# Copying neighbourhood q and k out of PSUM in one ScalarE pass, with scaled minima for row maxima, and three pieces of preparation work put elsewhere

## The chip, the cores and the metric

The kernel runs on one core of one Trainium2 chip. The metric is the device time of one execution in microseconds; lower is better. Several executions were timed, and one more was run under the hardware profiler, which gives the rows shown below. The engines are PE (TensorE: matmuls and, as PEld, weight loads), DVE (VectorE), ACT (ScalarE), POOL (GpSimd) and SP (SyncE, which here only issues DMAs).

## The reference

One transformer block on 1024 tokens of width 1024, batch 1. The tokens form a grid of 16 rows by 64 columns.

```python
h = layer_norm(x)
proj = h @ w_in + b_in                       # 1024 x 4352
qa, ka, va, qb, kb, vb, ga, gb = split(proj)
y_na  = neighbourhood_attention(qa, ka, va, rpb) @ w_branch_na   # 8 heads of 64, 8 x 16 window, bias
y_swa = windowed_gqa_with_sink(qb, kb, vb, sink) @ w_branch_swa  # 8 heads of 64, |i-j| <= 128, rotary
mixed = sigmoid(ga) * y_na + sigmoid(gb) * y_swa
h = layer_norm(2**.25 * h + mixed @ w_out + b_out)
u = square(relu(h @ w_ff1 + b_ff1))          # width 4096
h = layer_norm(2**.25 * h + u @ w_ff2 + b_ff2)
```

In the windowed attention the softmax has one more logit for each head, the sink. Its row maximum is the larger of the scores' maximum and the sink.

## The kernel before

All is float32 outside. For accuracy each operand of a product is split in a high and a low part, and a product is three matmuls: high by high, high by low, low by high. The first half of the program uses the type fp32r, the feed-forward layers use fp16 parts. `PE` is meant to run without a pause: everything else (splitting weights, copying out of PSUM, softmax, norms) is laid beside the matmuls by hand, in the order in which the Python code issues it (`manual_schedule` for all five engines). Each engine works through its own list in that order, so an instruction that waits holds up all behind it on its engine.

The stages that the change touches, in order of time:

**Attention (about 85 to 400 us).** One generator, `fill`, yields the projection matmuls one at a time; `pump(n)` issues n of them. `steps(s, n)` is one step of attention: the scores of step s+2 (`part_a`), a quarter of the n pumped matmuls, the exponentials of s+2 (`part_e`), the low parts of s+1 and their DMA transpose (`part_l`), 45% of the matmuls, the product with v of step s-1 (`part_c`), and the rest. A head is four steps; heads 0 to 7 are windowed heads, 8 to 15 neighbourhood heads. Work with a delay is put in a list by `defer(k, f, ...)`: f is issued at the first `flush` after k more pumped matmuls, and a flush marked early takes only what is marked early.

`proj_na_qk(h, ...)` is the projection of one neighbourhood head's q and k, in two halves of 512 tokens. Each half is 24 matmuls into one PSUM bank with tag "mm" (two banks have that tag). Rows 0 to 63 of the bank are q, rows 64 to 127 are k. `evac` copies q out once and k twice on ACT (high parts), `evac2`, deferred by D_NA = 4 matmuls, makes the low parts on DVE out of the same bank, which is free only after that. The score of a tile is then two matmuls of 128 rows: `q` (high over low) with `kh` (high twice), and `q` with `kl` (low twice). `part_a` adds bias or mask on DVE and takes row maxima with one `tensor_tensor_reduce` for each of two tiles into `st`; a `tensor_scalar` makes the negated scaled maxima `nm` from them (with the sink from `snk8`), and ACT's exponential reads `nm` as its bias.

**Output product and first norm (about 565 to 670 us).** For each of eight groups g of 128 tokens: two times 24 matmuls (`out_mm`), the residual added and statistics on DVE (`out_evac`), then `ln1_norm(g)`: the power for 1/std on POOL (L1366), a product on POOL (L174), the normalisation `z` on ACT (L176). In group g+1 PE turns group g (`turn`, 8 transposes at L1377). Two POOL jobs stand between: `bound`, seven small operations that need one small matmul's sum and give the scale `g1s` that `turn_evac` reads, and `late(i)`, four 128x512 POOL operations (L1529) that prepare the residual rows of group i.

**First feed-forward layer (about 665 to 962 us).** 16 column blocks p, each seven products of 12 matmuls in the order of `STEPS`: 1, 2, 6, 5, 7, 3, 4 (a Strassen-like scheme, banks a, b and c). After 1, 6 and 5 ACT takes a snapshot `sn` of the bank (L1614), before the bank's next product may be added to it. Beside them ACT and DVE prepare weights up to seven products ahead (`prep_to`), and ACT squares a whole raw weight block (`squares1`, 128x2048) to find its scale. For the second layer's first column group the four raw weight blocks are loaded by `load2` and squared by `squares2`, at the products that `LOAD2` and `SQUARE2` name as (p, product); `umax` and `scale2` make the scale out of these.

Of the kernel before, what the change touches and what calls it, by code (L numbers as in the profile page):

```python
# [10 lines left out]
F32 = mybir.dt.float32  # L11
F32R = mybir.dt.float32r
# [4 lines left out]
P = 128  # L17
# [73 lines left out]
def encoder_block(ctx, tc, x, w_in, w_br, w_out, w_ff1, w_ff2, par, rows, rpbp,  # L91
# [4 lines left out]
    def b32(ap):  # L96
        return ap.bitcast(F32)
# [90 lines left out]
    nc.scalar.dma_start(ident, ident_d)  # L188
    prm = cp.tile([P, N_PAR], F32, name="prm")
    nc.sync.dma_start(prm, par)  # L190
    snk8 = cp.tile([P, 8], F32, name="snk8")

    def bound_sets():
        for t, v in ((ones, 1.0), (pw[:, 0:1], -0.5), (pw[:, 1:2], 0.5), (cv, W_TOP ** -2), (hx[:, 4:6], 0.5),
# [98 lines left out]
    def h_perm(part, k, half):  # L293
        return hT[:, part, k, half * 512:(half + 1) * 512]
# [17 lines left out]
    def gemm3_steps(ps, w, act):  # L312

        hi, lo = w[:2]
        for k in range(NK):
            for i, (a, b) in enumerate(((hi, 0), (hi, 1), (lo, 0))):
                yield
                PE.matmul(ps, a[:, k, :], act(b, k), start=(k == 0 and i == 0), stop=(k == NK - 1 and i == 2))  # L318
# [92 lines left out]

    def proj_na_qk(h, w, store):
        q = ap.tile([P, S], F32R, tag="q", name="q", bufs=3)
        kh = ap.tile([P, S], F32R, tag="kh", name="kh")
        kl = ap.tile([P, S], F32R, tag="kl", name="kl")
        store.append((q, kh, kl))
        bq, bk = prm[0:64, C_QK + h:C_QK + h + 1], prm[64:P, C_QK + h:C_QK + h + 1]
        for half in range(2):
            cs = slice(half * 512, (half + 1) * 512)
            ps = psum("mm")  # L420
            yield from gemm3_steps(ps, w, lambda part, k: h_perm(part, k, half))

            def evac(cs=cs, ps=ps):
                ACT.activation(q[0:64, cs], ps[0:64, :], AF.Identity, bias=bq, scale=1.0)
                ACT.activation(kh[64:P, cs], ps[64:P, :], AF.Identity, bias=bk, scale=1.0)
                ACT.activation(kh[0:64, cs], ps[64:P, :], AF.Identity, bias=bk, scale=1.0)

            def evac2(cs=cs, ps=ps):
                DVE.scalar_tensor_tensor(out=q[64:P, cs], in0=ps[0:64, :], scalar=bq, in1=b32(q[0:64, cs]),
                                         op0=ALU.add, op1=ALU.subtract)  # L430
                DVE.scalar_tensor_tensor(out=kl[64:P, cs], in0=ps[64:P, :], scalar=bk, in1=b32(kh[64:P, cs]),  # L431
                                         op0=ALU.add, op1=ALU.subtract)
                DVE.tensor_copy(kl[0:64, cs], b32(kl[64:P, cs]))
            defer(0, lambda: (evac(), defer(D_NA, evac2, early=step_now[0] >= 32)), early=True)


    mk = ap.tile([P, 640], F32, tag="mk", name="mk", bufs=1)
# [182 lines left out]
    def part_a(s):  # L620

        hd, t = heads[s // 4], s % 4
        (q, kh, kl), _, _, bias_of, sink_h, o_chunk, o_row = hd.get()
        if t == 0 and o_row == 0:
            sums_l[o_chunk] = ap.tile([P, 2, 8], F32, tag="sl", name="sl", bufs=3)
            sums_s[o_chunk] = ap.tile([P, 2, 8], F32, tag="sk", name="sk", bufs=3)
        st = ap.tile([P, 2], F32, tag="st", name="st", bufs=4)
        nm = sums_s[o_chunk][:, o_row // 64, 2 * t:2 * t + 2]
        e = ap.tile([P, 768], F32, tag="ss", name="ss", bufs=2)
        tiles, at = [], 0  # L630
        for i in range(2):
# [4 lines left out]
            PE.matmul(ps[:, :n], q[:, j * P:(j + 1) * P], kh[:, c0 * P:c1 * P], start=True, stop=False)
            PE.matmul(ps[:, :n], q[:, j * P:(j + 1) * P], kl[:, c0 * P:c1 * P], start=False, stop=True)
            DVE.tensor_tensor_reduce(out=e[:, at:at + n], in0=ps[:, :n], in1=bias_of(j), scale=1.0, scalar=NEG,
                                     op0=ALU.add, op1=ALU.max, accum_out=st[:, i:i + 1])
            tiles.append((at, n, c0))  # L640
            at += n
        if sink_h is None:
            DVE.tensor_scalar(out=nm, in0=st, scalar1=-0.125, scalar2=None, op0=ALU.mult)  # L643
        else:
            DVE.tensor_scalar(out=nm, in0=st, scalar1=snk8[:, sink_h:sink_h + 1],
                              scalar2=-0.125, op0=ALU.max, op1=ALU.mult)
        hd.pairs[t] = e, tiles, at, nm
        if s > 0:
            rope_step(nm[:, 0:1])

    def part_e(s):

        if s >= 64:
            return
        hd, t = heads[s // 4], s % 4
        e, tiles, n_all, nm = hd.pairs[t]
        _, _, _, _, sink_h, o_chunk, o_row = hd.get()
        hh = o_row // 64
# [136 lines left out]
    with tc.manual_schedule(engines=MANUAL):  # L795
# [38 lines left out]
        for i in range(2 * NK + LAG + HB):  # L834
# [698 lines left out]
    with tc.manual_schedule(engines=MANUAL):  # L1533
# [6 lines left out]
        bound_squares()  # L1540
        for g in range(3, NCG):
            late_load(g)
        late(2)
        for g in range(NCG):
            out_mm(g, 0, 0, 8)
            if 2 <= g + 1 < NCG:
# [40 lines left out]
            if g == 5:
                op_places("S1", "S2")
            if g:
# [345 lines left out]
        for n, (p, i) in enumerate(seq):  # L1935
# [345 lines left out]
```

## Time and profile before

| what | us |
|---|---|
| three timed executions | 1263.60, 1264.92, 1265.20; median 1264.92 |
| the profiled execution: its own time | 1264.63 |
| the profiled execution: span from first to last instruction | 1262.8 |
| busy time of PE / DVE / ACT / POOL | 1235.7 / 960.0 / 797.0 / 321.3 |
| mean granted TensorE clock | 0.997 of full speed |

The profiled execution's own time is 1.8 us more than its span. A row of the timeline is: start, length in us, engine, line, operation, output<-inputs, shape, count; in brackets, how long the engine idled before it and what it waited for. A matmul's modelled end lies behind the start of the next one, since they are pipelined: what a matmul costs in a stream is the distance from its start to the next start.

### The profile page before, as it was taken

To read this page: it belongs to the slowest core of one execution; us is meant where nothing else is said; L and a number is where in the kernel's file an instruction comes from. 1 tells how busy PE (TensorE), PEld (TensorE's weight loads), DVE (VectorE), ACT (ScalarE), POOL (GpSimd) and SP (SyncE) were. 2 spreads that over 40 slices of the span, in tenths; PEclk is the share of its full clock that TensorE was granted. 3 is DMA by queue.
4 is the path that set the end of the run, shared out by engine and by line. 5 is a ranking of instruction groups with operands and counts; after the bars stand their busy time and mean duration, and the time that the engine had idled before them with its cause. 6 is when DMAs were issued, how large, how long until landed. Compare 5 with 4: busy or idle time off the path is not lost.

```text
span 1262.8 us, 16643 instructions
## 1 busy us (share of the span) xinstructions
PE 1235.7 (98%) x5954; PEld 796.4 (63%) x5954; DVE 959.9 (76%) x1409; ACT 797.0 (63%) x1280; POOL 321.3 (25%) x314
## 2 busy tenths in 40 slices
PE   8999999999999999999999999999999999999997
PEld 6788887877778778887884444444444444444443
DVE  7667889778778984443788977877757777898888
ACT  6448878677665455432567877787777746434457
POOL 4352331313110002436530013432300002211217
PEclk9999999999999999999999999999999999999999
DMA  6435667465476236546333456666927635363333
GB/s 238 158 143 132 153 152 176 105 159 131 110 165 200 73 134 202 199 133 243 124 150 109 138 188 217 209 204 205 335 90 266 226 134 225 125 257 127 125 109 133
DMA packets 166066, 211.55 MB, mean 168 GB/s; under 512 B 110432, under 2 KB 112224, under 8 KB 159712
## 3 DMA queue, kind: packets, MB, share of 16 engines
q1 hardware_dynamic: 165152, 209.72, 51.8%
q8 instruction: 46, 0.75, 0.2%
q10 hardware_dynamic: 832, 0.79, 0.2%
q14 instruction: 36, 0.29, 0.1%
HBM read 128.59 MB, written 56.18 MB: 146 GB/s over the span
## 4 chain that ended last, share of the span: by engine, by line
PE 72%; DVE 12%; ACT 7%; issue 3%; POOL 3%; DMA 2%; SPq 1%; POOLq 0%; DVEq 0%; ACTq 0%
PE ps_mm L318 17%; PE ps_o L1516 6%; PE ps_s L1986 6%; PE ps_mm L1986 6%; PE ps_t L1516 5%; PE ps_mm L1516 5%; PE ps_t L1986 5%; PE ps_o L1986 5%; PE ps_o L746 2%; PE ps_s L1516 2%; PE ps_mm L979 2%; PE ps_o L310 1%; PE ps_o L309 1%; PE ps_t L310 1%; PE ps_t L309 1%
## 5 line engine op out<-in xcount | busy, mean ns | idle before, releaser
L318 PE MATMUL ps_mm<-hT,whi 128*128 128x512 f32 x832 | 269.7, 398 | 7.1 <-DVE kl L431 4.5
L1516 PEld LDWEIGHTS <-tw 128*128 128x128 f16 x1248 | 122.5, 99 | 148.3 <-issue 5.8
L318 PEld LDWEIGHTS ps_mm<-hT,whi 128*128 128x128 f32 x832 | 155.2, 188 | 41.4 <-ACT ss L661 3.9
L1986 PEld LDWEIGHTS <-hS 128*128 128x128 f16 x1008 | 98.7, 98 | 118.2
L318 PE MATMUL ps_mm<-hT,wlo 128*128 128x512 f32 x416 | 165.5, 398 | 1.0 <-DVE wlo L812 1.0
L661 ACT ACTIVATE ss<-ss,sk 128x384 f32<-128x384 f32 (+1 forms) x128 | 74.3, 582 | 58.9 <-DVE sk L643 34.9
L1516 PE MATMUL ps_t<-hS,tw 128*128 128x512 f16 x384 | 88.1, 379 | 0.2
L318 PEld LDWEIGHTS ps_mm<-hT,wlo 128*128 128x128 f32 x416 | 78.3, 188 | 14.0 <-DVE wlo L812 1.5
L1271 POOL TENSOR_TENSOR mx<-sg 128x512 f32<-128x512 f32 x16 | 33.5, 2096 | 175.6 <-DVE sg L1270 175.6
L1704 DVE TENSOR_TENSOR usl<-usl 128x512 f32<-128x512 f32 x64 | 52.5, 821 | 27.1 <-ACT usl L1632 26.9
L1437 POOL TENSOR_TENSOR c<-c 128x2 f32<-128x2 f32 x16 | 16.8, 1056 | 199.3 <-DVE c L1436 199.3
L2006 POOL TENSOR_TENSOR acc<-acc,rst 128x512 f32<-128x512 f32 x16 | 32.8, 2051 | 121.5 <-DMA rst<-xr_d 113.7
L1986 PEld LDWEIGHTS <-hA 128*128 128x128 f16 x336 | 32.8, 98 | 39.7
L673 DVE SCALAR_TENSOR_TENSOR pl<-ss,pl 128x640 f16<-128x640 f32 (+1 forms) x64 | 57.1, 892 | 0.6 <-ACT pl L664 0.3
L1819 DVE SCALAR_TENSOR_TENSOR hS<-stg,c,hS 128x2048 f16<-128x2048 f32 x21 | 49.9, 2378 | 7.6 <-ACT hS L1816 7.6
L1443 DVE SCALAR_TENSOR_TENSOR tw<-raw,c,tw 128x512 f16<-128x512 f32 x60 | 51.1, 852 | 5.9 <-ACT tw L1440 5.9
L664 ACT ACTIVATE pl<-ss 128x640 f16<-128x640 f32 (+1 forms) x64 | 50.6, 791 | 3.0 <-DMA pt<-pl 1.0
L746 PE MATMUL ps_o<-pt,vv 128*128 128x256 f16 (+1 forms) x448 | 49.8, 251 | 0.0
L1516 PE MATMUL ps_o<-hS,tw 128*128 128x512 f16 x192 | 45.4, 388 | 2.1 <-ACT sn L1614 2.1
L444 POOL TENSOR_SCALAR tb<-tb 128x384 f32<-128x384 f32 x8 | 11.1, 1386 | 140.1 <-DMA tb<-in_rpbp 74.0
L1440 ACT ACTIVATE tw<-raw,c 128x512 f16<-128x512 f32 x60 | 41.4, 709 | 2.8 <-DVE raw L1481 2.8
L1986 PE MATMUL ps_mm<-hA,hS 128*128 128x512 f16 x192 | 42.9, 379 | 0.0
(386 smaller groups left out, 3001.2 us busy)
## 6 DMA issues: line engine op xcount, KB each, us to landing
us_d<-usl SPq DMA_DIRECT2D x112, 256.0 KB, 3.1
stg<-us_d SPq DMA_DIRECT2D x28, 1024.0 KB, 4.9
raw<-in_w_in SPq DMA_DIRECT2D x28, 512.0 KB, 4.0
raw<-in_w_ff SPq DMA_DIRECT2D x24, 512.0 KB, 5.7
sg<-sg_d SPq DMA_DIRECT2D x32, 256.0 KB, 3.0
hA<-in_w_ff SPq DMA_DIRECT2D x8, 1024.0 KB, 8.3
hS<-in_w_ff SPq DMA_DIRECT2D x8, 1024.0 KB, 8.1
sg_d<-sa SPq DMA_DIRECT2D x16, 256.0 KB, 2.3
```

What stands on the lines that cost most here:

```text
L318: PE.matmul(ps, a[:, k, :], act(b, k), start=(k == 0 and i == 0), stop=(k == NK - 1 and i == 2))
L661: ACT.activation(p, p, AF.Exp, bias=nm[:, i:i + 1], scale=0.125, accum_out=sums_l[o_chunk][:, hh, 2 * t + i:2 * t + i + 1])
L664: ACT.activation(pl[:, 0:n_all], e[:, 0:n_all], AF.Copy, bias=0.0, scale=P_SCALE)
L673: DVE.scalar_tensor_tensor(out=pl[:, n:2 * n], in0=e[:, 0:n], scalar=P_SCALE, in1=pl[:, 0:n], op0=ALU.mult, op1=ALU.subtract)
L746: PE.matmul(o, vs, move(part), start=(m == 0 and part == 0), stop=(m == len(runs) - 1 and part == 1))
L1271: POOL.tensor_tensor(out=mx[:, f, half * 512:(half + 1) * 512], in0=both[0], in1=both[1], op=ALU.add)
L1440: ACT.activation(hi_lo(slot, 0), src, AF.Copy, bias=0.0, scale=w_scale(p))
L1443: DVE.scalar_tensor_tensor(out=hi_lo(slot, 1), in0=src, scalar=w_scale(p), in1=hi_lo(slot, 0), op0=ALU.mult, op1=ALU.subtract)
L1516: PE.matmul(ps, ww, act[:, part, k, :], start=(first and k == 0 and m == 0), stop=(k == 3 and m == 2), skip_group_check=True)
L1704: DVE.tensor_tensor(out=out, in0=a, in1=b, op=op)
L1819: DVE.scalar_tensor_tensor(out=slot[:, :, 1, :], in0=src, scalar=scale, in1=slot[:, :, 0, :], op0=ALU.mult, op1=ALU.subtract)
L1986: PE.matmul(ps, st[:, a, part, j * P:(j + 1) * P], w[:, a, wpart, :], start=(first and a == 0 and m == 0), stop=(a == 3 and m == 2), skip_ ...
```

## The change

- `proj_na_qk`: the projection's columns are now k first, then q. One ACT pass copies the whole bank with its bias into an SBUF tile `qf` (tags "wlo2" and "vt"), which frees the bank. One matmul later, at the next flush, three ACT copies (`hi`) make q's high part twice and k's high part once out of `qf`; four matmuls later two DVE subtractions (`lo`) make the low parts. `kh` now holds k's high part over its low part, `q` holds q's high part twice, and the third tile, 64 rows of q's low part. The second score matmul of neighbourhood heads contracts over 64 rows, not 128.
- `part_a`: the reduction scales by -0.125 and takes minima, starting at minus the sink (`snk`), straight into `nm`; the `tensor_scalar` after it is gone, and the exponential scales by -1.
- First norm: `late(2)`, ahead of the first group before, and `late(3)` come one group later, and `bound`'s operations come after `ln1_norm(0)`.
- First feed-forward layer: the second layer's first four raw blocks are loaded at p = 5, 7, 9, 11 and squared at (6,7), (8,7), (10,7), (12,7); `umax(0)` and `scale2(0, ...)` come seven products earlier.

```diff
@@ proj_na_qk
-        store.append((q, kh, kl))
+        kk = ap.tile([P, S], F32R, tag="kh", name="kh")
+        ql = ap.tile([P, S], F32R, tag="kl", name="kl")
+        store.append((q, kk, ql))
...
-            def evac(cs=cs, ps=ps):
-                ACT.activation(q[0:64, cs], ps[0:64, :], AF.Identity, bias=bq, scale=1.0)
-                ACT.activation(kh[64:P, cs], ps[64:P, :], AF.Identity, bias=bk, scale=1.0)
-                ACT.activation(kh[0:64, cs], ps[64:P, :], AF.Identity, bias=bk, scale=1.0)
-            def evac2(cs=cs, ps=ps):
-                DVE.scalar_tensor_tensor(out=q[64:P, cs], in0=ps[0:64, :], scalar=bq, in1=b32(q[0:64, cs]), ...)
-                DVE.scalar_tensor_tensor(out=kl[64:P, cs], in0=ps[64:P, :], scalar=bk, in1=b32(kh[64:P, cs]), ...)
-                DVE.tensor_copy(kl[0:64, cs], b32(kl[64:P, cs]))
-            defer(0, lambda: (evac(), defer(D_NA, evac2, early=step_now[0] >= 32)), early=True)
+            def evac(ps=ps, half=half, b=b):
+                b.append((ap if half else wp).tile([P, 512], F32, tag="vt" if half else "wlo2", name="qf", bufs=1))
+                ACT.activation(b[0], ps, AF.Identity, bias=prm[:, C_QK + h:C_QK + h + 1], scale=1.0)
+            def hi(cs=cs, b=b):
+                ACT.copy(q[64:P, cs], b[0][64:P])
+                ACT.copy(kk[0:64, cs], b[0][0:64])
+                ACT.copy(q[0:64, cs], b[0][64:P])
+            def lo(cs=cs, b=b):
+                DVE.tensor_tensor(out=ql[0:64, cs], in0=b[0][64:P], in1=b32(q[64:P, cs]), op=ALU.subtract)
+                DVE.tensor_tensor(out=kk[64:P, cs], in0=b[0][0:64], in1=b32(kk[0:64, cs]), op=ALU.subtract)
+            defer(0, lambda evac=evac, hi=hi, lo=lo: (evac(), defer(1, hi, D_NA, lo, early=step_now[0] >= 32)),
+                  early=True)
@@ part_a
-            PE.matmul(ps[:, :n], q[:, j * P:(j + 1) * P], kl[:, c0 * P:c1 * P], start=False, stop=True)
-            DVE.tensor_tensor_reduce(out=e[:, at:at + n], in0=ps[:, :n], in1=bias_of(j), scale=1.0, scalar=NEG,
-                                     op0=ALU.add, op1=ALU.max, accum_out=st[:, i:i + 1])
+            if sink_h is None:
+                PE.matmul(ps[:, :n], kl[0:64, j * P:(j + 1) * P], kh[0:64, c0 * P:c1 * P], start=False, stop=True)
+            else:
+                PE.matmul(ps[:, :n], q[:, j * P:(j + 1) * P], kl[:, c0 * P:c1 * P], start=False, stop=True)
+            DVE.tensor_tensor_reduce(out=e[:, at:at + n], in0=ps[:, :n], in1=bias_of(j), scale=-0.125,
+                                     scalar=-NEG if sink_h is None else snk[:, sink_h:sink_h + 1],
+                                     op0=ALU.add, op1=ALU.min, accum_out=nm[:, i:i + 1])
-        if sink_h is None:
-            DVE.tensor_scalar(out=nm, in0=st, scalar1=-0.125, scalar2=None, op0=ALU.mult)
-        else:
-            DVE.tensor_scalar(out=nm, in0=st, scalar1=snk8[:, sink_h:sink_h + 1],
-                              scalar2=-0.125, op0=ALU.max, op1=ALU.mult)
@@ first norm
-        late(2)
+        LATE = {0: (2,), 1: (3, 4), 2: (5,), 3: (6,), 4: (7,)}
...
+            ps = bound_sum() if g == 0 else None
+            ln1_norm(g)
             if g == 0:
-                bound(bound_sum())
-            ln1_norm(g)
+                bound(ps)
...
-            if g < 5:
-                late(g + 3)
+            for i in LATE.get(g, ()):
+                late(i)
@@ first feed-forward layer
-        LOAD2 = {(12, 1): 0, (12, 6): 1, (12, 7): 2, (13, 1): 3}
-        SQUARE2 = {(13, 2): 0, (13, 5): 1, (13, 3): 2, (14, 1): 3}
+        LOAD2 = {(5, 1): 0, (7, 1): 1, (9, 1): 2, (11, 1): 3}
+        SQUARE2 = {(6, 7): 0, (8, 7): 1, (10, 7): 2, (12, 7): 3}
```

What the order of the instructions shows at three places (names as in the code; a row's L is its line in its own kernel; "x2" is two in a row).

ACT at the first neighbourhood head's first half, before. The three rows from `ps_mm` are `evac`; L661 are exponentials, L664 the copy of the probabilities to fp16:

```order
L580 CAST whi<-raw 128x1024
L752 COPY oT<-ps_o 64x512
L424 ACTIVATE q<-ps_mm,prm 64x512
L425 ACTIVATE kh<-ps_mm,prm 64x512
L426 ACTIVATE kh<-ps_mm,prm 64x512
L661 ACTIVATE ss,sl<-ss,sk 128x384
L661 ACTIVATE ss,sl<-ss,sk 128x256
L664 ACTIVATE pl<-ss 128x640
```

The same place of ACT in the changed kernel:

```order
L582 CAST whi<-raw 128x1024
L752 COPY oT<-ps_o 64x512
L425 ACTIVATE qf<-ps_mm,prm 128x512
L661 ACTIVATE ss,sl<-ss,sk 128x384
L661 ACTIVATE ss,sl<-ss,sk 128x256
L664 ACTIVATE pl<-ss 128x640
L428 CAST q<-qf 64x512
L429 CAST kh<-qf 64x512
L430 CAST q<-qf 64x512
```

Only one row reads the bank now, and the split into high parts has moved behind the exponentials and the fp16 copy.

POOL at the start of the output product, before. `zl` is `late`, the rows on `c` are `bound`, and `mv` is `ln1_norm(0)`:

```order
L1529 TENSOR_TENSOR zl<-zl 128x512 x4
L212 TENSOR_TENSOR c_5408<-c_5408 128x2
L213 TENSOR_SCALAR c_5408<-c_5408 128x1
L214 TENSOR_SCALAR c_5408<-c_5408 128x1
L216 TENSOR_TENSOR c_5408<-c_5408 128x1
L217 TENSOR_TENSOR c_5408<-c_5408 128x1
L218 TENSOR_SCALAR c_5408<-c_5408 128x1
L219 TENSOR_SCALAR c_5408<-prm,c_5408 128x16
L1366 TENSOR_TENSOR mv<-mv,mhalf 128x1
L174 TENSOR_SCALAR mv<-mv 128x1
L1529 TENSOR_TENSOR zl<-zl 128x512 x4
L1366 TENSOR_TENSOR mv<-mv,mhalf 128x1
```

The same place in the changed kernel:

```order
L1366 TENSOR_TENSOR mv<-mv,mhalf 128x1
L174 TENSOR_SCALAR mv<-mv 128x1
L212 TENSOR_TENSOR c_5296<-c_5296 128x2
L213 TENSOR_SCALAR c_5296<-c_5296 128x1
L214 TENSOR_SCALAR c_5296<-c_5296 128x1
L216 TENSOR_TENSOR c_5296<-c_5296 128x1
L217 TENSOR_TENSOR c_5296<-c_5296 128x1
L218 TENSOR_SCALAR c_5296<-c_5296 128x1
L219 TENSOR_SCALAR c_5296<-prm,c_5296 128x16
L1529 TENSOR_TENSOR zl<-zl 128x512 x4
L1366 TENSOR_TENSOR mv<-mv,mhalf 128x1
L174 TENSOR_SCALAR mv<-mv 128x1
```

The two rows of the first group's norm now stand ahead of everything else.

ACT in block p = 12 of the first feed-forward layer, before, from the snapshot after product 5 on (`junk` are the squares, `tw` weight high parts, `usl` the activation):

```order
L1614 ACTIVATE sn<-ps_t,prm,c_5408 128x512
L1426 ACTIVATE junk,c_5408<-raw 128x2048
L1440 ACTIVATE tw_6443<-raw,c_5408 128x512
L1440 ACTIVATE tw_5407<-raw,c_5408 128x512
L1637 ACTIVATE usl<-usl 128x512
L1638 ACTIVATE usl,c_5408<-usl 128x512
```

The same place in the changed kernel:

```order
L1615 ACTIVATE sn<-ps_t,prm,c_5296 128x512
L1426 ACTIVATE junk,c_5296<-raw 128x2048
L1440 ACTIVATE tw_6331<-raw,c_5296 128x512
L1829 ACTIVATE junk,c_5296<-hS_5879 128x2048
L1440 ACTIVATE tw_5295<-raw,c_5296 128x512
L1638 ACTIVATE usl<-usl 128x512
L1639 ACTIVATE usl,c_5296<-usl 128x512
```

A second pass over 2048 columns now stands there (the same holds in p = 6, 8 and 10), and four such passes are gone from p = 13 and 14.

More of the change, by code (lines that the diff above doesn't have):

```diff
@@ L190, in encoder_block @@
     nc.sync.dma_start(prm, par)
-    snk8 = cp.tile([P, 8], F32, name="snk8")
+    snk = cp.tile([P, 8], F32, name="snk")
     def bound_sets():
@@ L413, in proj_na_qk @@
         q = ap.tile([P, S], F32R, tag="q", name="q", bufs=3)
-        kh = ap.tile([P, S], F32R, tag="kh", name="kh")
-        kl = ap.tile([P, S], F32R, tag="kl", name="kl")
-        store.append((q, kh, kl))
-        bq, bk = prm[0:64, C_QK + h:C_QK + h + 1], prm[64:P, C_QK + h:C_QK + h + 1]
+        kk = ap.tile([P, S], F32R, tag="kh", name="kh")
+        ql = ap.tile([P, S], F32R, tag="kl", name="kl")
+        store.append((q, kk, ql))
         for half in range(2):
@@ L421, in proj_na_qk @@
             yield from gemm3_steps(ps, w, lambda part, k: h_perm(part, k, half))
-            def evac(cs=cs, ps=ps):
-                ACT.activation(q[0:64, cs], ps[0:64, :], AF.Identity, bias=bq, scale=1.0)
-                ACT.activation(kh[64:P, cs], ps[64:P, :], AF.Identity, bias=bk, scale=1.0)
-                ACT.activation(kh[0:64, cs], ps[64:P, :], AF.Identity, bias=bk, scale=1.0)
-            def evac2(cs=cs, ps=ps):
[L429 to L432, printed above, removed]
-                DVE.tensor_copy(kl[0:64, cs], b32(kl[64:P, cs]))
-            defer(0, lambda: (evac(), defer(D_NA, evac2, early=step_now[0] >= 32)), early=True)
+            b = []
+            def evac(ps=ps, half=half, b=b):
[10 more added lines that the diff above has]
+                  early=True)
     mk = ap.tile([P, 640], F32, tag="mk", name="mk", bufs=1)
@@ L626, in part_a @@
             sums_s[o_chunk] = ap.tile([P, 2, 8], F32, tag="sk", name="sk", bufs=3)
-        st = ap.tile([P, 2], F32, tag="st", name="st", bufs=4)
         nm = sums_s[o_chunk][:, o_row // 64, 2 * t:2 * t + 2]
@@ L660, in part_e @@
             p = e[:, at:at + n]
-            ACT.activation(p, p, AF.Exp, bias=nm[:, i:i + 1], scale=0.125,
+            ACT.activation(p, p, AF.Exp, bias=nm[:, i:i + 1], scale=-1.0,
                            accum_out=sums_l[o_chunk][:, hh, 2 * t + i:2 * t + i + 1])
@@ L847, in encoder_block @@
             if i == NK:
-                POOL.tensor_scalar(out=snk8, in0=prm[:, C_S:C_S + 8], scalar1=8.0, scalar2=None, op0=ALU.mult)
+                POOL.tensor_scalar(out=snk, in0=prm[:, C_S:C_S + 8], scalar1=-1.0, scalar2=None, op0=ALU.mult)
                 residual_rows()
@@ L1948, in encoder_block @@
                 scale1(n // 3, sum_sq1(n // 3, "s"))
-            if (p, i) == (14, 5):
+            if (p, i) == (13, 5):
                 scale2(0, sum_sq2(0, "s"))
@@ L1957, in encoder_block @@
                 squares2(0, SQUARE2[p, i])
-            if (p, i) == (13, 6):
+            if (p, i) == (12, 6):
                 umax(0)
@@ L2233 @@
     b_in = a["b_in"][0]
-    qk = np.concatenate([b_in[0:512].reshape(8, 64).T, b_in[512:1024].reshape(8, 64).T], axis=0)
+    qk = np.concatenate([b_in[512:1024].reshape(8, 64).T, b_in[0:512].reshape(8, 64).T], axis=0)
     par = np.concatenate([
@@ L2257 @@
     w = a["w_in"][0]
-    w = np.concatenate([w[:, 0:1024].reshape(D, 2, 8, 64).transpose(0, 2, 1, 3).reshape(D, 1024), w[:, 1024:]], axis=1)
+    w = np.concatenate([w[:, 0:1024].reshape(D, 2, 8, 64)[:, ::-1].transpose(0, 2, 1, 3).reshape(D, 1024), w[:, 1024:]], axis=1)
     w_in = w.reshape(8, 128, 34, 128).transpose(2, 1, 0, 3)
```

## The prediction

> **What bounds the kernel.** I read the page's first two parts, then PE's own waits, then the timeline around each long one.
>
> ```profile
> PE 1235.7 (98%) x5954; PEld 796.4 (63%) x5954; DVE 959.9 (76%) x1409; ACT 797.0 (63%) x1280; POOL 321.3 (25%) x314
> ```
>
> PE is busy for 98% of the span of 1262.8, and no other engine over 76%. Making DVE or ACT cheaper is therefore worth only what PE waits for them; the whole stake is PE's 27 us of idle time and what its matmuls cost. Who makes PE wait (total us, times, longest):
>
> ```profile
> PE ps_mm L318 <- DVE kl L431: 4.5, 7, 1.0
> PE ps_t L1377 <- ACT z L176: 3.1, 2, 2.8
> PE ps_o L1516 <- ACT sn L1614: 2.1, 1, 2.1
> ```
>
> These are the three longest entries, and all three are places that the change touches; the rest of PE's idle time is mostly the program's start and its tail, which it leaves alone. Two of the stages (busy us and counts of each engine, the granted clock, the DMA share):
>
> ```profile
> core 0: us, PE busy (x) PEld busy (x) DVE busy (x) ACT busy (x) POOL busy (x), PEclk, DMA share, GB/s
> 200.00:360.00 160.00, 155.55 (x836) 125.40 (x835) 127.91 (x273) 118.38 (x236) 40.44 (x64) 1.00 0.57 138
> 900.00:940.00 40.00, 37.77 (x172) 17.32 (x170) 24.90 (x44) 33.00 (x55) 5.58 (x5) 0.96 0.55 203
> ```
>
> **Part 1, neighbourhood q and k.** One of the seven waits, on three engines:
>
> ```profile
> 218.79 0.39 PE L318 MATMUL ps_mm<-hT,wlo 128*128 128x512 f32 x1
> 220.20 0.70 PE L318 MATMUL ps_mm<-hT,whi 128*128 128x512 f32 x2 [1.02 <-DVE kl L431]
> ...
> 216.42 0.68 ACT L424 ACTIVATE q<-ps_mm,prm 64x512 fp32r<-64x512 f32 x1
> ...
> 218.53 0.75 DVE L429 SCALAR_TENSOR_TENSOR q<-ps_mm,prm,q 64x512 fp32r<-64x512 f32 x1 [1.24 <-ACT kh L426]
> 219.29 0.76 DVE L431 SCALAR_TENSOR_TENSOR kl<-ps_mm,prm,kh 64x512 fp32r<-64x512 f32 x1
> ...
> 39.51 50.41 PE ps_mm L318 x220
> ```
>
> The bank is held from 216.42 to 220.05: three ACT passes of 0.68, then two DVE passes that wait for the third (kh, L426). In a stream a matmul of 512 columns costs 50.41/220 = 0.23, so this stall costs 1.41 - 0.23 = 1.18, 0.16 more than the 1.02 in brackets. Seven of them: 4.5 + 7 x 0.16 = 5.6. What the new pieces cost, from like rows (the windowed heads already have such a copy-out with a later split):
>
> ```profile
> L480 ACT ACTIVATE qf<-ps_mm,prm x10: 674/689/691, 52.8 to 157.1; 128x512 f32<-128x512 f32 x10
> L536 ACT CAST q<-qf x16: 605/616/620, 80.6 to 179.5; 64x512 fp32r<-64x512 f32 x16
> L541 DVE TENSOR_TENSOR q<-qf,q x16: 684/687/1673, 81.6 to 181.3; 64x512 fp32r<-64x512 f32 x16
> L645 DVE TENSOR_SCALAR sk<-st,snk x32: 228/229/355, 91.5 to 215.1; 128x2 f32<-128x2 f32 x32
> L643 DVE TENSOR_SCALAR sk<-st x32: 168/169/342, 221.5 to 393.6; 128x2 f32<-128x2 f32 x32
> ```
>
> The bank is now free after one ACT pass, 0.69 after ACT comes to it instead of 3.63: at about 217.1 where PE asks for it at 219.0. That leaves 1.9 us, and the other six stalls were shorter still, so all seven go: **-5.6**. ACT pays 0.69 + 3 x 0.62 = 2.54 for each half where it paid 3 x 0.68 = 2.05: 16 x 0.49 = 7.8 more in a stage where it is busy for 118.4 of 160. DVE pays 2 x 0.69 = 1.38 where it paid 0.75 + 0.76 = 1.51 and one copy more: at least 16 x 0.13 = 2 less of 127.9. Both are hidden under PE, ACT at 126 of 155 us. If that cover goes, the copy-out would have to come 1.9 us late before PE sees it. The split itself comes later: its casts stand behind two exponentials and the fp16 copy, so DVE's subtractions, which wait for them, end about 0.5 later than before, and what is behind them on DVE (the next row maxima) with them. The scores of that head are two to three steps of 5.5 us away, so PE does not see this.
>
> The row maxima drop 32 operations of 0.23 and 32 of 0.17 on DVE, none on PE's path: 0. In the windowed heads the reduction now takes its start from a column; L645 against L643 prices such a column at 0.06, less than the 0.23 it saves.
>
> The 64-row matmul is the one cost on PE itself. No row of the trace shows one. It streams the same columns, so a gain is excluded. Bounds for entering and leaving another tile shape:
>
> ```profile
> 222.13 0.83 PE L746 MATMUL ps_o<-pt,vv 128*128 128x256 f16 x8
> ...
> 223.04 0.62 PE L318 MATMUL ps_mm<-hT,whi 128*128 128x512 f32 x2
> ...
> 224.19 0.34 PE L636 MATMUL ps_s<-kh,q 128*128 128x384 f32 x1
> 224.36 0.34 PE L637 MATMUL ps_s<-kl,q 128*128 128x384 f32 x1
> ...
> 227.66 0.83 PE L746 MATMUL ps_o<-pt,vv 128*128 128x256 f16 x8
> 228.33 0.27 PE L698 MATMUL ps_t<-ident,rl 128*16 128x128 f32 x1
> ...
> 228.68 0.63 PE L318 MATMUL ps_mm<-hT,whi 128*128 128x512 f32 x2
> ...
> 588.19 1.09 PE L1377 MATMUL ps_t<-ident,z 128*128 128x128 f32 x8 [2.77 <-ACT z L176]
> 589.04 0.48 PE L1348 MATMUL ps_s<-wo,m 128*128 128x512 f32 x1
> ```
>
> The lower end: the transpose L698 uses 16 of 128 array columns. With it, the stretch from L746 to L318's second group takes 1.02, without it 0.91: 0.11, and a full-shape transpose costs (589.04 - 588.19)/8 = 0.11 as well. The excursion costs nothing. [...] I take the near row, the only one with a change of shape, and allow what four times rounded to 0.01 cannot exclude, 0.02 for each: 64 x 0.02 = **+1.3**. [...]
>
> **Part 2, the first norm.**
>
> ```profile
> 585.03 0.39 PE L1350 MATMUL ps_s<-wo,m 128*128 128x512 f32 x1
> ...
> 578.75 0.15 DVE L1365 TENSOR_SCALAR mv<-mv 128x1 f32<-128x1 f32 x1
> ...
> 577.84 5.28 POOL L1529 TENSOR_TENSOR zl<-zl 128x512 f32<-128x512 f32 x4 [7.70 <-DMA zl<-xr_d]
> ...
> 585.93 0.56 POOL L1366 TENSOR_TENSOR mv<-mv,mhalf 128x1 f32<-128x1 f32 x1
> ...
> 586.82 6.23 POOL L1529 TENSOR_TENSOR zl<-zl 128x512 f32<-128x512 f32 x4
> 594.32 0.55 POOL L1366 TENSOR_TENSOR mv<-mv,mhalf 128x1 f32<-128x1 f32 x1 [1.28 <-DVE mv L1365]
> ...
> 586.89 1.24 ACT L176 ACTIVATE z<-z,mv 128x1024 f32<-128x1024 f32 x1 [20.58 <-POOL mv L174]
> ```
>
> The statistics are ready at 578.9, but POOL is in `late(2)`, which waited for its load, until 583.1, and then in `bound` until 585.9. PE stands from 585.26 to 588.19: 2.93. With the power first, z is done at 578.9 + 0.9 + 1.24 = 581.1, 4 us before PE asks. `bound` then ends at about 583, ahead of the copies that read it, and `late(2)` at 583 + 5.3 = 588.5, ahead of group 2's first half near 593. Next in line: `late(3)` and `late(4)` run from about 592.3 (594.32 - 2.93 + 0.9) for 2 x 6.23 to 604.8; the third group's statistics come one group of 48 x 0.23 + 8 x 0.11 = 11.9 after the second's, at 603.3, so its power waits 1.5 us and z is done at 606.9, while PE turns it at 585.26 + 2 x 11.9 = 609.1. So 2 us are left, and the whole stall goes: **-2.9**. No DMA changes its place here.
>
> **Part 3, squares of the second layer.**
>
> ```profile
> 925.04 2.75 PE L1516 MATMUL ps_s<-hA,tw 128*128 128x512 f16 x12
> 929.90 4.13 PE L1516 MATMUL ps_o<-hS,tw 128*128 128x512 f16 x12 [2.10 <-ACT sn L1614]
> ...
> 927.20 1.89 ACT L1828 ACTIVATE junk<-hS 128x2048 fp8e5<-128x2048 f32 x1
> ...
> 902.15 0.63 ACT L1637 ACTIVATE usl<-usl 128x512 f32<-128x512 f32 x1 [0.18 <-DVE usl L1634]
> ...
> 904.10 0.78 ACT L1631 ACTIVATE usl<-ps_mm,prm,c 128x512 f32<-128x512 f32 x1 [0.56 <-PE ps_mm L1516]
> ...
> 906.69 0.78 ACT L1614 ACTIVATE sn<-ps_mm,prm,c 128x512 f32<-128x512 f32 x1 [0.45 <-PE ps_mm L1516]
> ```
>
> The snapshot that PE waits for stands right behind the last of four squares. The stall is 2.10 + 0.16 = 2.3, and after it 12 matmuls take 4.13 instead of 2.75; the granted clock was 0.96 over the 40 us from 900, and 0.04 x 40 = 1.6, of which I count 1.5. [...] Without these four passes, 4 x 1.9 of ACT's 33 busy in 40 us, the stall goes: **-3.8**.
>
> They now stand in p = 6, 8, 10, 12, a second pass one weight copy behind the one that is there already. In p = 12 that adds 1.9 ahead of the last three rows above; their idle times 0.18, 0.56 and 0.45 take up 1.2, so the snapshot of 906.69 comes 0.8 late and ends at 908.3. PE adds to that bank again after product 2, 2.6 after product 1 ended at 906.7: at 909.3. One us is left, so I cost this at 0. The loads move from p = 12 and 13 to odd p; SP issues them behind the same pair of raw loads, and each has one block more to land before it is squared. `scale2` comes seven products earlier with its inputs.
>
> **Sum**, against the profiled execution's 1264.63 (the median of the others, 1264.92, is 0.3 above): -5.6 - 2.9 - 3.8 = -12.3, +1.3 for the tile shapes: 1253.6. Without the 1.3 it is 1252.3.
>
> **Rivals.**
> - [...] 128 changes; the gain is eaten at 12.3/128 = 0.096 each. [...] For it speaks that no row shows a 64-row tile, against it L698. 0.09 in all: 0.06 slower than before, 0.03 between.
> - *The squares stall four blocks.* The us of slack in p = 12 is used up if a load or DVE holds ACT by as much again. Each stall of 1 us, with slow matmuls of 1.5 behind half of them: 4 x 1 + 2 x 1.5 = 7, so 1260.6; with short stalls alone 4 x 0.5 = 2, so 1255.6. The slack is thin; against it, PE lost nothing in the blocks before 13, each with one such pass. 0.15.
> - *The bank still comes late.* Then ACT, not DVE, would be what held it, and part 1 returns nothing: 1259.2. Against it, the 1.9 us above. 0.10.
>
> **How the numbers follow.** The forecast has 0.66; its own range is 1250.5 to 1257, from no cost of the 64-row tiles and a further us or two of small waits that go, to 0.05 for each change. The range 1250 to 1261 leaves out the drain and the worst of the others. A change under 0.2%, 2.5 us, can't be told from none: "same" reaches from 1262 to 1267. Faster: 0.66 + 0.14 + 0.09 = 0.89; slower 0.06, same 0.05.
>
> **What would show it.** Right: PE's waits no longer list the low part at the bank, nor z, nor sn, and each such stage has PE busy all through; PEclk stays at 1.00 where the blocks 13 and 14 run. A 64-row score matmul is followed by the next after 0.17 to 0.19. Wrong: that distance at 0.3 or more, a new PE row "<- ACT qf", or several "<- ACT sn" between p = 6 and 12.

## The result and the profile after

The changed kernel takes 1277.9 us (median of four, 1277.6 to 1278.8) against 1264.9 us before: a ratio of 1.011, interval 1.009 to 1.012. It is 13 us slower, where 1253.6 was forecast. The page of the changed kernel, and what PE waits for (total us, times, longest):

```profile
PE 1256.7 (98%) x5954; PEld 796.8 (62%) x5954; DVE 957.8 (75%) x1329; ACT 804.2 (63%) x1296; POOL 310.6 (24%) x314
```

```profile
PE ps_mm L318 <- POOL hT L290: 2.1, 4, 1.1
PE ps_t L1377 <- ACT z L176: 1.9, 1, 1.9
```

These two are now the longest entries. The seven waits for the bank and the wait for the snapshot are gone from the list, as forecast. Of the two for z, the one at group 0 is gone, and the one at group 7 has grown from 0.3 to 1.9. PE still issues 5954 matmuls, and its busy time has grown by 21 us: the loss is not in its waits but in the matmuls. The windows (busy us and counts of each engine, granted clock, DMA share):

```profile
core 0: us, PE busy (x) PEld busy (x) DVE busy (x) ACT busy (x) POOL busy (x), PEclk, DMA share, GB/s
200.00:360.00 160.00, 160.00 (x773) 116.63 (x772) 108.20 (x212) 116.76 (x233) 37.28 (x56) 1.00 0.54 125
900.00:940.00 40.00, 40.00 (x193) 18.78 (x191) 30.89 (x49) 32.07 (x57) 12.73 (x10) 1.00 0.56 193
```

In 160 us of the score stage PE is now busy without a gap, and yet it gets through 773 matmuls where it got through 836 before. The timeline around one score step of a neighbourhood head shows why, first PE, then its weight loads:

```profile
285.71 0.62 PE L318 MATMUL ps_mm<-hT,whi 128*128 128x512 f32 x2
286.17 0.34 PE L637 MATMUL ps_s<-kh,q 128*128 128x384 f32 x1
286.44 0.44 PE L639 MATMUL ps_s<-kh,kl 64*128 64x384 f32 x1
286.81 0.38 PE L637 MATMUL ps_t<-kh,q 128*128 128x256 f32 x1
287.12 0.38 PE L639 MATMUL ps_t<-kh,kl 64*128 64x256 f32 x1
287.43 0.50 PE L318 MATMUL ps_mm<-hT,wlo 128*128 128x512 f32 x1
287.76 0.63 PE L318 MATMUL ps_mm<-hT,whi 128*128 128x512 f32 x2
```

```profile
285.94 0.19 PEld L637 LDWEIGHTS ps_s<-kh,q 128*128 128x128 f32 x1
286.44 0.18 PEld L639 LDWEIGHTS ps_s<-kh,kl 64*128 64x128 f32 x1 [0.31 <-issue]
286.80 0.19 PEld L637 LDWEIGHTS ps_t<-kh,q 128*128 128x128 f32 x1 [0.18 <-issue]
287.12 0.18 PEld L639 LDWEIGHTS ps_t<-kh,kl 64*128 64x128 f32 x1
287.43 0.19 PEld L318 LDWEIGHTS ps_mm<-hT,wlo 128*128 128x128 f32 x1
```

L637 loads its weights at 285.94, beside the projection's last matmul, 0.23 ahead of its own start. From the first 64-row matmul on (L639, "64*128") every load in these rows starts at the very time of its own matmul, and the distances from start to start are 0.27, 0.37, 0.31, 0.31 and 0.33, where a stream of full-row matmuls of the same columns has 0.17, 0.17, 0.12, 0.12 and 0.23: 0.78 lost in a step, and there are 32 such steps, 25 us.

To place the rest I add up, for each stretch of the program, how much each distance from start to start exceeds the median of matmuls of its column count and type in the trace before. For the whole program that excess is 30.9 before and 44.3 after; the difference of 13.4 is the whole change of the span (1276.2 - 1262.8). By place: the score stage (the matmuls of 210 to 395 us in the trace before) from 8.9 to 27.4 (+18.5), the turn of group 0 from 3.0 to 0 (-3.0), the turn of group 7 from 0.5 to 2.1 (+1.6), the snapshot with the slow matmuls behind it from 4.1 to nothing (-4.2), and a wait near 106 us from 0.3 to 0.8 (+0.5).

The wait at group 7 is not new: PE idled there for 0.29 before (at 671.74) and idles for 1.90 now. ACT at that place, before and then after, with one row of DVE and of PE:

```profile
651.39 1.91 ACT L1426 ACTIVATE junk<-hS 128x2048 fp8e5<-128x2048 f32 x1 [0.92 <-DMA hS<-in_w_ff]
...
655.97 1.23 ACT L176 ACTIVATE z<-z,mv 128x1024 f32<-128x1024 f32 x1
```

```profile
669.00 1.91 ACT L1426 ACTIVATE junk<-hS 128x2048 fp8e5<-128x2048 f32 x1 [2.41 <-DMA hS<-in_w_ff]
...
673.41 1.23 ACT L176 ACTIVATE z<-z,mv 128x1024 f32<-128x1024 f32 x1
...
675.18 0.69 DVE L1394 TENSOR_TENSOR hS<-s2t,hS 128x512 f16<-128x512 f32 x1 [3.31 <-ACT hS L1393]
...
689.19 1.09 PE L1377 MATMUL ps_t<-ident,z 128*128 128x128 f32 x8 [1.90 <-ACT z L176]
```

ACT's squares of the head blocks 2 and 3 stand ahead of group 6's normalisation (the second row) and wait 2.41 instead of 0.92 for their load. PE comes 15.8 us later to the turn of group 5 than before (663.46 against 647.63), but this normalisation comes 17.4 later (673.41 against 655.97). DVE idles for 3.31 until ACT's casts behind it are done, where it idled for 2.39 before, and what DVE still has to do for group 7 is late by that: part of what PE gained at group 0 is lost again here.

### The profile page after: what moved, and what is told of

It reads as the page before. It is cut to its first block, busy times and chain, and to the rows that moved or that the text cites. A ratio compares the mean times of both kernels' runs of the same rounds, so it can differ in the third digit from the quotient of the medians.

```text
span 1276.2 us, 16575 instructions
## 1 busy us (share of the span) xinstructions
PE 1256.7 (98%) x5954; PEld 796.8 (62%) x5954; DVE 957.8 (75%) x1329; ACT 804.2 (63%) x1296; POOL 310.6 (24%) x314
## 4 chain that ended last, share of the span: by engine, by line
PE 86%; DVE 7%; ACT 3%; POOL 2%; issue 1%; DMA 1%; POOLq 0%; DVEq 0%; ACTq 0%
PE ps_mm L318 22%; PE ps_o L1516 6%; PE ps_t L1516 6%; PE ps_mm L1987 6%; PE ps_s L1987 6%; PE ps_mm L1516 5%; PE ps_t L1987 5%; PE ps_o L1987 4%; PE ps_o L746 3%; PE ps_s L1516 2%; PE ps_mm L979 2%; PE ps_t L637 1%; PE ps_o L308 1%; PE ps_t L308 1%; PE ps_o L310 1%
## 5 line engine op out<-in xcount | busy, mean ns | idle before, releaser
L318 PE MATMUL ps_mm<-hT,wlo 128*128 128x512 f32 x416 | 169.4, 407 | 1.3 <-DVE wlo L812 1.0
L661 ACT ACTIVATE ss<-ss,sk 128x384 f32<-128x384 f32 (+1 forms) x128 | 74.3, 582 | 40.9 <-DVE sk L642 40.3
L673 DVE SCALAR_TENSOR_TENSOR pl<-ss,pl 128x640 f16<-128x640 f32 (+1 forms) x64 | 71.9, 1124 | 1.7 <-ACT pl L664 1.4
L664 ACT ACTIVATE pl<-ss 128x640 f16<-128x640 f32 (+1 forms) x64 | 50.6, 791 | 11.1 <-DMA pt<-pl 9.5
L642 DVE CUSTOM_DVE_ANT_0 ss<-ps_s,bm 128x384 f32<-128x384 f32 (+1 forms) x32 | 16.7, 522 | 49.5 <-PE ps_s L639 49.4
```

The source lines that it names most:

```text
L661: ACT.activation(p, p, AF.Exp, bias=nm[:, i:i + 1], scale=-1.0, accum_out=sums_l[o_chunk][:, hh, 2 * t + i:2 * t + i + 1])
L673: DVE.scalar_tensor_tensor(out=pl[:, n:2 * n], in0=e[:, 0:n], scalar=P_SCALE, in1=pl[:, 0:n], op0=ALU.mult, op1=ALU.subtract)
```

## Experiments

**1. full_rows: the change with 128 rows.**

```diff
+ DVE.tensor_tensor(out=ql[64:P, cs], in0=b[0][64:P], in1=b32(q[64:P, cs]), op=ALU.subtract)
...
- PE.matmul(ps[:, :n], kl[0:64, j * P:(j + 1) * P], kh[0:64, c0 * P:c1 * P], start=False, stop=True)
+ PE.matmul(ps[:, :n], kl[:, j * P:(j + 1) * P], kh[:, c0 * P:c1 * P], start=False, stop=True)
```

> The kernel after, but the second score matmul of a neighbourhood block runs over all 128 rows again: the low part of q is written to both halves of its tile (16 DVE subtractions of 64x512 more, 0.69 each, 11 us on an engine that is busy for 108 of 160), so that the product also takes in q_lo x k_lo. Theory (rows): in the trace after, a 64-row matmul among 128-row ones starts 0.146 later than a 128-row one would, and the matmul behind it 0.191 later, and where that is a projection its next 0.11 later: 64 x 0.337 + 32 x 0.11 = 25 us. Then this kernel takes 1277.9 - 25 = 1253, and the distances are back at 0.117 and 0.173. Rival (stage): something else that the change put into the score stage holds PE, for instance a bank or ACT's longer copy-out, and the rows have nothing to do with it: 1275 to 1278. Between the two, if only part of the 18.5 us lost in that stage hangs on the rows.

Measured: 1256.2 us, ratio to before 0.993 (0.992 to 0.995), 9.3 below the 1265.5 of the kernel before in the same set; 21.7 less than the changed kernel. A score step of it on PE:

```profile
280.16 0.34 PE L638 MATMUL ps_s<-kh,q 128*128 128x384 f32 x1
280.33 0.34 PE L640 MATMUL ps_s<-kh,kl 128*128 128x384 f32 x1
280.51 0.28 PE L638 MATMUL ps_t<-kh,q 128*128 128x256 f32 x1
280.62 0.28 PE L640 MATMUL ps_t<-kh,kl 128*128 128x256 f32 x1
280.75 0.40 PE L318 MATMUL ps_mm<-hT,wlo 128*128 128x512 f32 x1
```

The distances are 0.17, 0.18, 0.11 and 0.13 again. So the rows cost the change its gain, and the rival (something else in the stage) falls. It missed 1253 by 3 us. Waits account for most of them: two entries for the score stage that the changed kernel does not have (the last two below), and 0.4 more at group 7, where the changed kernel waits 1.9:

```profile
PE ps_t L1378 <- ACT z L176: 2.3, 1, 2.3
...
PE ps_o L747 <- DVE oT L756: 1.3, 2, 0.8
...
PE ps_mm L318 <- ACT qf L425: 0.6, 1, 0.6
```

**2. before_half: the kernel before, with 64 rows alone.**

```diff
+ r = slice(0, 64 if sink_h is None else P)
- PE.matmul(ps[:, :n], q[:, j * P:(j + 1) * P], kl[:, c0 * P:c1 * P], start=False, stop=True)
+ PE.matmul(ps[:, :n], q[r, j * P:(j + 1) * P], kl[r, c0 * P:c1 * P], start=False, stop=True)
```

> The kernel before, with one edit: the second score matmul of each neighbourhood block takes only rows 0 to 63 of its operands, which leaves out the product of the two low parts. No instruction is added, removed or moved. Theory (rows): 64 such matmuls cost 0.337 each and 32 of them 0.11 more behind them: 1264.9 + 25 = 1290; a little less if the seven waits for the bank (5.6 us) shrink because PE comes later. Rival (stage): 1265, since nothing else of the change is in it.

Measured: 1284.5 us, ratio 1.015 (1.014 to 1.017), +19. That is 25 less the bank waits, which all but vanish, although the old copy-out, which holds the bank for five passes of ACT and DVE, still stands:

```profile
PE ps_mm L318 <- DVE kl L431: 0.2, 1, 0.2
```

A PE that is late by 0.78 a step no longer meets a full bank. So the empty list of bank waits in the profile after proves nothing for the new copy-out; it must be read from full_rows.

**3. adjacent: as many 64-row matmuls, half the changes.** The edit in short form:

```diff
- for i in range(2): PE.matmul(... 128 rows, tile i); PE.matmul(... 64 rows, tile i)
+ for i in range(2): PE.matmul(... 128 rows, tile i)
+ for i in range(2): PE.matmul(... 64 rows, tile i)
```

> The kernel after, with the four score matmuls of a neighbourhood step in another order: both 128-row ones, then both 64-row ones. As many 64-row matmuls (64), half as many changes of row count (64 instead of 128). Theory (change): the cost hangs on the change, because the weight load of the next matmul is not done beside the running one when the row count differs; then one exit and one entry a step go, 32 x (0.191 + 0.146) = 10.8 us: 1267. Rival (each): every 64-row matmul pays for itself whatever stands beside it, for instance because its own load never runs ahead: 1278.

Measured: 1264.6 us, ratio to before 0.9995 (0.9986 to 1.0004); 13.3 less than the changed kernel. PE, then its loads:

```profile
275.90 0.33 PE L640 MATMUL ps_t<-kh,q 128*128 128x384 f32 x1
276.17 0.44 PE L643 MATMUL ps_s<-kh,kl 64*128 64x384 f32 x1
276.45 0.33 PE L643 MATMUL ps_t<-kh,kl 64*128 64x384 f32 x1
276.71 0.50 PE L318 MATMUL ps_mm<-hT,wlo 128*128 128x512 f32 x1
277.05 0.39 PE L318 MATMUL ps_mm<-hT,whi 128*128 128x512 f32 x1
```

```profile
276.17 0.18 PEld L643 LDWEIGHTS ps_s<-kh,kl 64*128 64x128 f32 x1 [0.25 <-issue]
276.28 0.19 PEld L643 LDWEIGHTS ps_t<-kh,kl 64*128 64x128 f32 x1
276.71 0.19 PEld L318 LDWEIGHTS ps_mm<-hT,wlo 128*128 128x128 f32 x1 [0.25 <-issue]
```

The second 64-row matmul loads at 276.28, beside the first: between equal row counts the load runs ahead, and only the two changes pay. Each shows in two distances. Medians over the 24 steps of 384 columns: entry 0.264 and exit 0.265 where 0.172 is normal, +0.09; and the distance behind the matmul that was entered is 0.281 instead of 0.172, behind the first projection matmul 0.333 instead of 0.23, +0.105. With 256 columns both are the same (0.210 and 0.207 against 0.117, then 0.224). So the price of a change is 0.09 + 0.105 = 0.195, with 256 columns as with 384: 128 changes make 25.0 us, 64 make 12.5, near the 13.3 of the times. The rival (each 64-row matmul pays for itself) falls.

**4. ff_half: 64 rows among fp16 matmuls.**

```diff
+ r = slice(0, 64 if 4 <= p < 12 and k == 1 and m == 2 else P)
- PE.matmul(ps, ww, act[:, part, k, :], ...)
+ PE.matmul(ps, ww[r], act[r, part, k, :], ...)
```

> The kernel before, with 56 fp16 matmuls of 512 columns in the first feed-forward layer (one of twelve in each product of eight weight blocks) cut to 64 rows, which leaves half of that contraction out; all else is as before. A weight load takes 0.188 for the fp32 tiles of the scores and 0.098 for these fp16 tiles. Theory (load): what a change of rows costs is the weight load that is no longer hidden, once on entry and once on exit; with fp16 that is about half, 0.05 to 0.1 in and 0.10 out, in all 56 x 0.15 to 0.2 = 8 to 11 us: 1273 to 1276. Rival (drain): the cost is a fixed emptying of the array, the same 0.34 to 0.38 whatever the type: 56 x 0.36 = 20 us, 1285. Third: no cost with fp16, 1265.

Measured: 1275.6 us, ratio 1.008 (1.007 to 1.010), +10. The loads around one of them:

```profile
795.81 0.31 PEld L1517 LDWEIGHTS <-tw 128*128 128x128 f16 x2
796.54 0.09 PEld L1517 LDWEIGHTS <-tw 64*128 64x128 f16 x1 [0.42 <-issue]
796.86 0.33 PEld L1517 LDWEIGHTS <-tw 128*128 128x128 f16 x3 [0.23 <-issue]
```

Medians of 56: entry 0.312 and exit 0.319 where 0.216 is normal, and 0.227 behind the exit. So the first part of a change, 0.096 and 0.103, is nearly the same for fp16 as for fp32; the second, 0.105 with the fp32 load of 0.188, is 0.01 with the fp16 load of 0.098. In all 0.21 for each matmul, 56 x 0.21 = 11.8. The time agrees best with the load theory, and the rows agree with it once the two parts are added: a change costs 0.195 with the load of 0.188 and 0.105 with the load of 0.098, in both types one whole weight load and 0.007. So a change can be read as one load that is no longer hidden, once on entry and once on exit, as that theory had it. It can also be read as 0.09 that is fixed and a rest that hangs on the load; for these two loads both come to the same sums. Which of them it is, and whether the array runs empty meanwhile, no run tells. The rival (0.36 for each matmul whatever the type) falls.

**5 to 7. The parts alone.** part1 is full_rows with the parts 2 and 3 taken back; part2 and part3 are the kernel before with that part of the diff.

> The kernel before with part 1 and the scaled minima alone, its second score matmul over all 128 rows (as in full_rows); the first norm and the squares stand as before. Forecast of the prediction: the seven waits for the bank go, -5.6: 1259.3. Theory now, from the trace of full_rows: that stage gives back 3.4 only, since two waits of 0.83 and 0.46 for DVE's move of the attention output (L756) and one of 0.6 for ACT's copy-out take the place of part of them, and 0.5 is lost near 105 us: 1264.9 - 2.9 = 1262. Rival, from before_half, where the seven waits also went while the old copy-out stood: the copy-out has no part in it, and with PE at its old pace the waits come back: 1265.

> The kernel before with part 2 alone (order of GpSimd's work after the first groups of the output product, and the norm ahead of the sum for the bound). Forecast of the prediction: the stall of 2.93 at the turn of group 0 goes: 1262.0. Theory now: of it 1.6 to 2 comes back at the turn of group 7, since ACT's two squares there wait for loads that do not come earlier with the rest, and group 6's normalisation, its casts, DVE's list behind them and group 7's normalisation stand behind those squares: -1.0 to -1.4, 1263.5 to 1263.9. Rival: that second stall comes from the other parts (PE's later or earlier arrival), and here the full 2.9 is seen.

> The kernel before with part 3 alone (loads and squares of the second layer in the blocks 5 to 12). Forecast of the prediction: stall 2.3 and slow matmuls 1.5, -3.8: 1261.1. Theory now: -2.4 to -2.5, 1262.4, and the 1.5 is not the change's: in before_half and in ff_half the same stall of 2.1 stands at the same place, and the matmuls behind it run at full pace (no excess over 900 to 920 us against 1.54 in the profile of before), so the half clock was of that one execution.

Measured, against 1264.5 for the kernel before in the same set: part1 1262.8 us, ratio 0.998 (0.997 to 0.999); part2 1261.4, ratio 0.998 (0.997 to 0.999); part3 1261.4, ratio 0.998 (0.997 to 0.999): -1.8, -3.2 and -3.2. Their sum, -8.2, is near full_rows' -9.3.

Of part1 the theory held (-2.9 expected; its interval reaches from -1.0 to -3.3): the seven waits go, and two for DVE's move of the attention output (1.6 in all) and one for the copy-out (0.4) come. Its rival falls: PE is at its old pace here, and the waits do not come back.

Of part2 the expectation failed by 2 us. The time is near its rival's 2.9, but the rival's reason is not there: the second wait, 1.8 at group 7, stands in the trace. A part of the 2 us may lie in the price of the stall that it takes away. The same stall at the turn of group 0, in the profile of part3:

```profile
587.27 1.97 PE L1377 MATMUL ps_t<-ident,z 128*128 128x128 f32 x8 [2.72 <-ACT z L176]
```

Here the eight transposes take 1.97 where they took 1.09 in the profile of before, behind the same wait, and the excess at this place is 4.3 instead of 3.0. The stall at the snapshot does the same the other way round; PE there in the profiles of part1 and of part2:

```profile
927.76 4.44 PE L1517 MATMUL ps_o<-hS,tw 128*128 128x512 f16 x12 [2.10 <-ACT sn L1615]
```

```profile
927.77 2.75 PE L1516 MATMUL ps_o<-hS,tw 128*128 128x512 f16 x12 [2.10 <-ACT sn L1615]
```

The same wait of 2.10, at the same time in the program to 0.01 us, is followed by slow matmuls in one execution and by full pace in the other; the granted clock from 927 to 934 was 0.76 in the first and 1.00 in the second. Of the five profiles that still have the stall of group 0 two show slow matmuls behind it, and of the five that have the snapshot's, two. (At group 7, the 2.43 that PE waits in adjacent are followed by them too.) A stall of 2 to 3 us thus costs itself and, in some executions, about 1.5 more (4.13 - 2.75 = 1.4 in before and 4.44 - 2.75 = 1.7 in part1 at the snapshot, 4.3 - 3.0 = 1.3 in part3 at group 0); one profile shows one draw. With 0.4 x 1.5 added to each as an estimate, part2 is worth 3.0 + 0.6 - 1.6 = 2.0 and part3 2.5 + 0.6 = 3.1, both inside their intervals (part2's reaches from -1.8 to -4.2); the rest of part2's 3.2, about 1, is not explained.

**8. mended.** full_rows, with ACT's squares behind group 6's normalisation, and q's low part copied by POOL. The edit, its second half in short form:

```diff
- DVE.tensor_tensor(out=ql[64:P, cs], in0=b[0][64:P], in1=b32(q[64:P, cs]), op=ALU.subtract)
+ POOL.tensor_copy(ql[64:P, cs], b32(ql[0:64, cs]))
...
- if g == 6: squares1(2), squares1(3)        # ahead of out_evac(6, 1)
+ if g == 6: squares1(2), squares1(3)        # behind combine(5)
```

> full_rows with two edits: ACT's squares of the head blocks 2 and 3 stand behind group 6's normalisation and casts instead of ahead of them; and the second copy of q's low part is made by GpSimd (a copy of 64x512) instead of a DVE subtraction. Theory: the turn of group 7 no longer waits (2.3 of PE, -2.0 against full_rows), and with DVE 11 us less busy the waits for its move of the attention output go (1.3 less their share in before, about -1): 1256.2 - 3 = 1253. Rival for the first: the raw loads, not the place of the squares, hold group 7, or the blocks' scales come late and PE waits for a weight slice instead: no gain. Rival for the second: GpSimd's bias masks (7 of 0.71 a head) hold the copies, and PE waits for the scores' operand: slower than full_rows.

Measured: 1254.9 us, ratio 0.992 (0.991 to 0.994), the lowest time here, though its interval overlaps that of full_rows: 9.7 and 9.3 below their own kernels before. The copy by POOL worked in the trace: the excess in the score stage falls from 5.5 in full_rows to 3.6, against 2.8 in mended2 below, where PE waits for nothing in that stage. The other place of the squares did not:

```profile
PE ps_t L1378 <- ACT z L176: 1.8, 1, 1.8
...
PE ps_o L1432 <- ACT junk L1427: 1.2, 1, 1.2
```

PE now waits 1.2 for the squares themselves, and 1.8 of the wait for group 7 stays. DVE's idle time has only moved one step on, to a weight copy that now stands behind the squares on ACT:

```profile
654.34 1.42 DVE L1444 SCALAR_TENSOR_TENSOR tw<-hA,c,tw 128x512 f16<-128x512 f32 x2 [3.25 <-ACT tw L1441]
```

**9. mended2.** mended, with the sum over these squares and what hangs on it (scales, weight splits) behind group 7's product and normalisation. The edit in short form:

```diff
  out_mm(7, 1, 4, 8)
+ head_ps += [sum_sq1(2), sum_sq1(3)]        # before: ahead of it
  out_evac(7, 1); ln1_norm(7)
+ scale1(2), scale1(3); head_split(2, ..)    # before: ahead of out_evac(7, 1)
```

> mended with one more edit in group 7: the sum over the squares of head blocks 2 and 3 stands behind the whole of group 7's output product instead of in its middle, and the scales and the split of these blocks' weights, which follow from it on GpSimd, ACT and DVE, stand behind group 7's normalisation instead of ahead of it. Theory: in mended PE waits 1.2 for the squares at that sum, and 1.8 at the turn of group 7, because DVE adds the last half of group 7's output only after the weight split, which waits for GpSimd's scale; both go: -1.2 - 1.5, 1254.9 - 2.7 = 1252.2. Rival: the normalisation is late for DVE's longer list behind group 6 anyway, or the split weights come late for the first products: no gain, 1255 or above.

Measured: 1257.2 us, ratio 0.994 (0.993 to 0.996): 2.3 more than mended, though the two intervals overlap a little. The rival's forecast came true (no gain, 1255 or above). Both waits went as planned, and PE runs on to the next:

```profile
673.03 5.09 PE L1517 MATMUL ps_s<-hA,twx 128*128 128x512 f16 x12 [4.37 <-DVE usl L1634]
```

DVE reaches the operation that PE waits for at 672.24, against 672.07 for the same operation in full_rows and 671.09 in mended. PE is earlier, and DVE is not: what holds PE at this place seems to be DVE's list of work, not the order of one wait in it, though no run makes that list shorter. The longer stall is followed by slow matmuls, 5.09 for these twelve where 2.75 is normal, which is as much as the kernel is slower than mended. A version without any wait there was not found.

## Why the prediction was wrong

- **The step that failed: the 64-row matmul, +1.3.** The rows measure 64 x 0.39 = 25.0. Taking L698 as the nearest row was the error: it is narrower in array columns, and there it costs nothing (0.11, as much as a full-shape transpose); fewer rows are another thing. A change of the row count costs 0.195, near the weight load of 0.188 that no longer starts ahead of its matmul, and twice the 0.096 at which the gain is eaten. That rival was right, and had a chance of 0.09 on one row of another kind. The drain that the range leaves out was the author's assumption, and no run shows it: the runs show the 0.195, of which 0.09 to 0.10 lies ahead of the next recorded start in both types, and not what that time is spent on.
- **Loads beside matmuls.** The prediction put nothing on the weight loads around a 64-row matmul, and so took them as hidden without a reason. The trace shows that in the score steps a load runs ahead between matmuls of equal row count only: by 0.11 to 0.23 from 128 to 128 rows in the changed kernel, by 0.17 from 64 to 64 in adjacent. Where the row count changes, it starts with its own matmul, at most 0.002 ahead in the changed kernel.
- **Part 1, -5.6.** The mechanism is right, the size depends on what DVE has to do besides. With full rows and 16 more DVE subtractions (part1) the kernel gains 1.8 in time and 2.9 in the stage; with POOL making that copy (mended) the stage's excess falls from 8.9 to 3.6, a gain of 5.3. In the changed kernel itself the seven waits would have all but gone without the new copy-out, since 64 rows alone leave 0.2 of them in before_half.
- **Part 2, -2.9.** The stall at group 0 went. What the prediction missed is the next one, at group 7, which stood before with 0.3: it followed POOL's queue and the turns of groups 1 and 2, and not ACT's squares at group 6 and the list of DVE behind them. The place of the squares is not the whole cause, since the wait stays when they are moved alone (mended). In the profile after -3.0 and +1.6; alone -3.2 in time.
- **Part 3, -3.8.** Right: the stall went, none of the blocks 6 to 12 loses more than 0.15, and alone it measures -3.2. The 1.5 for the slow matmuls was counted as certain; they stand in two of five profiles (the twelve matmuls behind the snapshot's stall took 4.13 and 4.44 in these, and 2.75 in the other three).
- **Row maxima, 0.** No wait points to them, and no run took them alone.

Summed with the measured terms: the kernel with full rows is 9.3 below before; the 128 changes add 25.0; what a slower PE no longer loses in the score stage, its waits above all, takes 3.1 back (full_rows' excess of 5.5 against 27.4 - 25.0 = 2.4 in the changed kernel): -9.3 + 25.0 - 3.1 = +12.6. Measured: +13.0; the kernel before alone differs by 0.6 between the two sets.

## What to carry to other kernels

Before shortening a matmul's contraction to save operand work, look at its neighbours: among full-row matmuls each change of the row count cost about one weight load here (0.195 with a load of 0.188 in fp32, 0.105 with one of 0.098 in fp16), so fill the idle rows (a second copy of the low part, made by an idle engine) or put the short ones side by side. When no row shows the thing that a change introduces, the nearest row must be near in the quantity that changes; if it is not, what it costs is no measure, and the range must be wide enough to say so. And when a wait disappears, ask whether its cause went or whether the waiting engine merely became slower: before_half lost nearly all of the same seven waits with the old code in place.

## What the runs showed of the hardware

- A change between 128 and 64 rows of the array costs PE 0.195 in fp32 (256 and 384 columns), with a weight load of 0.188, and 0.105 in fp16 (512 columns), with a load of 0.098. Of this, 0.09 to 0.10 shows in the distance to the next recorded start and the rest, 0.105 and 0.01, in the distance behind it; the load starts with its own matmul instead of ahead of it.
- Between two 64-row matmuls the load runs ahead, 0.17 in adjacent, where 0.17 is usual between 128-row ones of the same 384 columns.
- In the changed kernel, in adjacent and in ff_half a 64-row matmul took no less than a full-row one of the same columns: the distance behind it was 0.26 to 0.37 with 384 columns in fp32 where 0.17 is normal, and 0.319 with 512 columns in fp16 where 0.216 is.
- A PE stall of 2.10 at the same place of the program was followed by twelve matmuls in 4.44 in one execution (granted clock 0.76 from 927 to 934) and in 2.75 in another (1.00); one of 2.72 by eight transposes in 1.97 (part3), and one of 2.77 by the same eight in 1.09 (before).
